# Key/value projections moved between the steps of a pass, and two sample-attention parts joined in one chain

## The chip, the core and the metric

The kernel runs on one core of a Trainium2 chip. The core has five engines that work through their own queues in order and meet at semaphores: TensorE (PE, matrix products and transposes into PSUM), VectorE (DVE), ScalarE (ACT), GpSimd (POOL) and SyncE (SP, which here only issues transfers). PSUM has 8 banks; products land there and ACT or DVE read them out. The metric is the device time of one execution in microseconds (us); the number given for a kernel is the median of its runs.

## The reference, cut to what matters

One inference step of a one-layer decoder is computed for two groups that share their weights: a prompt of 512 rows and eight sample rows, each with 1024 cached rows. All inputs are float32. The mixer, to which the change belongs, computes from the normed rows pooling channels, queries, three branches of keys and values (compressed, selected, window) and gates:

```python
z = rmsnorm(x, g_mix) @ w_in
u = z[..., :o1]
q = z[..., o1:o2].reshape(B, T, N_HEADS, HEAD_DIM)
kv = z[..., o2:o3].reshape(B, T, N_BRANCH, 2, KV_HEADS, HEAD_DIM)
gates = jax.nn.sigmoid(z[..., o3:]).reshape(B, T, N_HEADS, N_BRANCH)
```

Attention over the three branches is weighted by the gates:

```python
p_c = masked_softmax(s_c, cmp_end[None, :] <= pos_q[:, None])     # compressed blocks of 32 rows
imp = jnp.einsum('bghtn,nj->bgtj', p_c, ovl)                      # importance of blocks of 64 rows
_, idx = lax.top_k(imp, k_sel)                                    # 16 blocks, three of them forced
o_s = ...                                                         # softmax over the selected blocks' rows
o_w = jnp.einsum('bghts,bsgd->btghd', p_w.astype(dt), kvw[:, :, 1])   # the last 512 rows
o = g[..., 0:1] * o_c + g[..., 1:2] * o_s + g[..., 2:3] * o_w
```

For the sample rows the cached rows come through a page table, and the selection leaves out one block of 17. After the mixer follow the output projection, cross attention into 256 memory tokens and a gated MLP. The new key and value rows are outputs too.

## The kernel before

Features lie on partitions. The 512 prompt rows and 8 sample rows form the columns of one operand, 2 x 260. To keep float32 accuracy each operand is split into a high and a low part (`split_w`, `split`: ACT copies the high part, line 111, DVE subtracts, line 114), and a projection of 128 output features (`project`, line 194) takes three products for each of 8 row blocks and two column halves: 48 products. Its result gathers in a pair of PSUM banks (`pp`).

The code is Python that is traced once. Generators mark with `yield cost` where another generator may go on, and `merge` runs several side by side in proportion to the costs that they yield. The trace order is a priority. A planner then fixes each engine's order at compile time by priority and by its own estimate of when an instruction's inputs are ready, and places a wait where a buffer is used again (`bufs` counts the buffers of a name). `open_pool` takes space from the left or the right end of SBUF, `open_psum` banks; a new pool over an old one's place waits tile by tile.

The stages around the change, in order:

- Query tiles (`q_tiles`): four projections, beside them the compressed branch's keys and values (`kv_tiles(0)`). Each query tile's result is at once split into `Qst`, eight heads of high and low parts, by ACT and DVE.
- The pass over the cached rows (`sample_pass`): 4 quarters (two batch rows each) of 8 steps. POOL gathers 1 MB of rows for two steps into one of three buffers (`ch_raw`, line 606). In each step `front` reorders them (`chg`), transposes keys (line 613) and the rows to be compressed (line 617), keeps the values (`Vh`) and splits the turned rows (`cx_hi`, `cx_lo`). `back` multiplies the step before with the compressing weights (line 429), accumulating over a quarter in a bank `s`, and every second step computes the selected branch's scores (line 639) into `Ssl`. At the end of a quarter `cmp_finish` reads the bank four times (ACT into `cmp_t`, DVE line 564 into `KC`, `VC`). Banks: two `s`, two `tk`, four `tb`.
- `s1_b` beside `sample_selected`. `s1_b` projects keys and values of the selected and window branches, four tiles; keys are split into `Ksl` and `Kwn` for the prompt's attention, and all are turned back (line 477) and stored. `sample_selected` is a chain: compressed probabilities, the block left out, a softmax over 1025 scores, transposes (line 728), products with the values (line 735).
- `pooling` beside `sample_window`. Pooling has four projections, sums over windows on POOL, four small products (line 840). `sample_window` loads keys and values of the window (`kw` with four buffers, `vw` with eight), turns the keys (line 899), takes scores (line 904), softmax, products (lines 928 and 932), and adds up the sample rows' attention in `ysel`. Its pool lies where `Vh` was.
- The prompt's attention (scores line 976) beside the pooling half of the output projection (line 865) and the memory's projection.

## Time and profile before

| | us |
|---|---|
| median of 3 runs | 923.21 |
| lowest and highest | 921.41, 924.14 |
| span of the profiled execution | 922.6 |
| query tiles, 34.9 to 62.8 | 27.9 |
| pass over the cached rows, 62.8 to 126.6 | 63.8 |
| key/value tiles beside the selected branch, 126.6 to 163.8 | 37.2 |
| pooling beside the window, 163.8 to 207.6 | 43.8 |

The profiled execution's span, from its first to its last instruction, is 0.6 us under the median of the runs. In rows of the profile PE is TensorE's products, PEld its weight loads, which overlap them, and SPq the transfers that SP issues. L194 is line 194 of the kernel. A row of a timeline gives start, duration, engine, line, operation, what is written and read, and in brackets how long the engine idled before and what ended that. A product's duration overlaps that of the next; the pace is the distance of starts. A busy PE therefore isn't a PE at its peak.

### The profile page before, as it was taken

How to read it: one execution, taken by the hardware profiler on the slowest of the kernel's cores; microseconds unless marked ns; L12 is line 12 of the kernel's file. 1: busy time of each engine (PE TensorE's matmuls, PEld its weight loads, DVE VectorE, ACT ScalarE, POOL GpSimd, SP SyncE). 2: the span in 40 equal slices, each digit the busy share in tenths (PEclk: the TensorE clock that was granted, in tenths of full speed). 3: DMA queues.
4: the chain of work that ended last, by engine and by line, in shares of the span. 5: the costliest groups of instructions: out<-in, count | busy, mean ns of one | idle time of the engine just before them, and what ended most of it. 6: DMA issues, size and time to landing. Idle time of an engine off the chain costs nothing.

```text
span 922.6 us, 17866 instructions
## 1 busy us (share of the span) xinstructions
PE 894.8 (97%) x7266; PEld 827.3 (90%) x7266; DVE 610.5 (66%) x1547; ACT 420.8 (46%) x794; POOL 90.5 (10%) x93
## 2 busy tenths in 40 slices
PE   7999999899999999999998999999999999999996
PEld 6997788788878768999888999999999999999995
DVE  5566676558876775788765368775357775357765
ACT  6657764136675665444433344443124443124432
POOL 2112200420000001300004200000000000000051
PEclk9999999999999999999999999999999999999998
DMA  7447753821133336647733453332333332333212
GB/s 206 154 137 267 246 181 100 240 59 49 47 97 110 115 99 185 222 142 247 251 126 100 160 178 106 92 96 91 90 92 92 92 96 92 90 94 93 78 52 93
DMA packets 125460, 118.99 MB, mean 129 GB/s; under 512 B 8985, under 2 KB 116413, under 8 KB 123251
## 3 DMA queue, kind: packets, MB, share of 16 engines
q1 hardware_dynamic: 121523, 94.02, 33.9%
q0 software_dynamic: 3824, 23.80, 7.2%
q8 instruction: 57, 0.93, 0.5%
q14 instruction: 24, 0.20, 0.1%
q10 hardware_dynamic: 32, 0.04, 0.0%
HBM read 111.75 MB, written 10.69 MB: 133 GB/s over the span
## 4 chain that ended last, share of the span: by engine, by line
PE 85%; DMA 7%; DVE 3%; ACT 2%; issue 1%; SPq 0%; DVEq 0%; ACTq 0%
PE ps_pp L194 57%; DMA ch_raw<-in_cache_kv_dram,ix_ch 3%; PE ps_tb L865 3%; PE ps_tb L1103 3%; PE ps_sc L976 3%; PE ps_o L1012 2%; DMA w_u<-in_w_up_dram 2%; PE ps_tb L1130 2%; PE ps_tf L1005 2%; PE ps_s L429 2%; DMA w_kv<-in_w_in_dram 1%; PE ps_x L1289 1%; PE ps_x L1270 1%; PE ps_tb L617 1%; PE ps_tb L639 1%; DVE w_lo L114 1%
## 5 line engine op out<-in xcount | busy, mean ns | idle before, releaser
L194 PE MATMUL ps_pp<-x_hi,w_lo 128*128 128x260 f32 x832 | 169.2, 284 | 0.5 <-DVE w_lo L114 0.5
L194 PE MATMUL ps_pp<-x_hi,w_hi 128*128 128x260 f32 x832 | 169.5, 284 | 0.0
L194 PE MATMUL ps_pp<-x_lo,w_hi 128*128 128x260 f32 x832 | 167.9, 283 | 0.0
L194 PEld LDWEIGHTS ps_pp<-x_hi,w_lo 128*128 128x128 f32 x832 | 128.7, 188 | 1.2 <-DVE w_lo L114 0.7
L194 PEld LDWEIGHTS ps_pp<-x_hi,w_hi 128*128 128x128 f32 x832 | 128.7, 188 | 0.4
L194 PEld LDWEIGHTS ps_pp<-x_lo,w_hi 128*128 128x128 f32 x832 | 128.1, 188 | 0.4 <-issue 0.4
L111 ACT ACTIVATE w_hi<-w_raw 128x1024 fp32r<-128x1024 f32 (+1 forms) x54 | 55.8, 1036 | 114.6 <-PE ps_pp L194 100.9
L114 DVE TENSOR_TENSOR hT<-hT,ps_pp 128x520 f32<-128x520 f32 (+1 forms) x42 | 28.1, 670 | 86.3 <-PE ps_pp L194 83.3
L111 ACT ACTIVATE w_hi<-w_u 128x1024 fp32r<-128x1024 f32 x44 | 46.7, 1061 | 76.0 <-PE ps_pp L194 64.9
L114 DVE TENSOR_TENSOR w_lo<-w_raw,w_hi 128x1024 fp32r<-128x1024 f32 (+1 forms) x54 | 66.7, 1236 | 8.3 <-ACT w_hi L111 8.1
L194 PE MATMUL ps_pp<-h_hi,w_hi 128*128 128x260 f32 x328 | 66.7, 284 | 0.0
L194 PE MATMUL ps_pp<-h_hi,w_lo 128*128 128x260 f32 x328 | 66.0, 282 | 0.0
L194 PE MATMUL ps_pp<-h_lo,w_hi 128*128 128x260 f32 x328 | 66.0, 282 | 0.0
L114 DVE TENSOR_TENSOR ext<-ps_pp,R 128x512 f32<-128x512 f32 x44 | 30.4, 691 | 45.3 <-PE ps_pp L194 45.1
L114 DVE TENSOR_TENSOR w_lo<-w_u,w_hi 128x1024 fp32r<-128x1024 f32 x44 | 53.9, 1226 | 6.8 <-ACT w_hi L111 6.5
L194 PEld LDWEIGHTS ps_pp<-h_hi,w_hi 128*128 128x128 f32 x328 | 50.6, 188 | 0.3 <-ACT h_hi L111 0.2
L194 PEld LDWEIGHTS ps_pp<-h_lo,w_hi 128*128 128x128 f32 x328 | 50.5, 188 | 0.0
L194 PEld LDWEIGHTS ps_pp<-h_hi,w_lo 128*128 128x128 f32 x328 | 50.5, 188 | 0.0
L194 PE MATMUL ps_pp<-xn_hi,w_hi 128*128 128x260 f32 x224 | 48.6, 296 | 0.4 <-ACT xn_hi L327 0.4
L261 POOL TENSOR_TENSOR acc<-hT 128x520 f32<-128x520 f32 x3 | 4.2, 1397 | 456.2 <-DVE hT L114 456.2
L194 PE MATMUL ps_pp<-xn_hi,w_lo 128*128 128x260 f32 x224 | 47.2, 289 | 0.5 <-DVE w_lo L114 0.5
L194 PE MATMUL ps_pp<-xn_lo,w_hi 128*128 128x260 f32 x224 | 46.8, 290 | 0.5 <-DVE xn_lo L330 0.5
(494 smaller groups left out, 2068.0 us busy)
## 6 DMA issues: line engine op xcount, KB each, us to landing
w_u<-in_w_up_dram SPq DMA_DIRECT2D x44, 512.0 KB, 5.3
xkr<-in_cache_mem_dram SPq DMA_DIRECT2D x16, 512.0 KB, 6.3
xvr<-in_cache_mem_dram SPq DMA_DIRECT2D x16, 512.0 KB, 5.1
w_raw<-in_w_down_dram SPq DMA_DIRECT2D x8, 1024.0 KB, 5.0
w_raw<-in_w_in_dram SPq DMA_DIRECT2D x4, 1024.0 KB, 5.3
w_raw<-in_w_xkv_dram SPq DMA_DIRECT2D x4, 1024.0 KB, 5.6
w_v<-in_w_xkv_dram SPq DMA_DIRECT2D x4, 1024.0 KB, 5.8
w_raw<-in_w_xq_dram SPq DMA_DIRECT2D x4, 1024.0 KB, 6.5
```

Source lines behind the costliest of these rows:

```text
L111: act.activation(o, i, AF.Copy, scale=scale)
L114: (eng or dve).tensor_tensor(o, a, b, op=op)
L194: pe.matmul(ps[:, hf, :HT], a[:, k, :], x[:, hf, :], start=(k == 0 and j == 0), stop=(k == kt - 1 and j == 2))
L429: pe.matmul(ps, w[:, c, j].rearrange("p i e -> p (i e)"), x, start=(first and j == 0 and q == 0), stop=(j == 7 and q == 2), skip_group_che ...
L617: pe.transpose(pt[:, a * P:(a + 1) * P], chg[:, a].rearrange("p s d -> p (s d)"), ident)
L639: pe.matmul(ps[32 * c:32 * c + 32, 0:256], Qbd[:, blk(r, c):blk(r, c) + 32], kt[:, i].rearrange("p t n -> p (t n)"), start=True, stop=True ...
L865: pe.matmul(ps[:, :HT], a[:, k, :], y[x][:, k, hf, :], start=(k + j == 0), stop=(k == 3 and j == 2))
L976: pe.matmul(ss_[hl][:, 0:c0 + nk], Qst[:, h, qc], k[:, g, u, 0:c0 + nk], start=(u == 0), stop=(u == 1))
L1005: pe.transpose(pt[:, hh * P:(hh + 1) * P], pr[hh][:, kb * P:(kb + 1) * P], ident)
L1012: pe.matmul(po[hp * 64:(hp + 1) * 64, g * 256:(g + 1) * 256], Vtok[:, br, kb - 1, g * 64:(g + 1) * 64], pTs[kb - 1][:, hp * 256:(hp + 1) * ...
L1103: pe.matmul(ps[:, 0:MEM], a[:, k, :], x[:, k, :], start=(k == 0 and j == 0), stop=(k == 7 and j == 2))
L1130: pe.matmul(ps[i], x[:, k, ts_], w[:, kl, :], start=(k == 0 and j == 0), stop=(k == KT - 1 and j == 2))
```

## The change

The four projections of the selected and the window branch's keys and values leave their own stage. They become `kv_rest`, which is merged with the pass, row block by row block (six products between two yields); the pass yields twice per step. Their weights come by 128 columns into one buffer of the pass's pool. The results stay in `zk` (keys) and `Vtok` (values); the split of the keys comes later (`split_keys`). For their PSUM pair the pass gives up one of its two `s` banks and one of four `tb` banks.

The selected branch, the key splits and the window now form one generator, `samples`, beside `pooling`, which yields after each row block. The window's pool opens when the selected branch is done.

The queries stay unsplit in `zq`; `split_queries` makes `Qst` after pooling, ahead of the prompt's attention. `kv_first` is the compressed branch's part of `kv_tiles`, with its turning in a `tb` bank. Comments are dropped throughout.

```diff
+    Vtok = ptile(at, [P, 2, NQB, P], "Vtok")
...
+    zq = ptile(smp, [P, 4, 2, HT], "zq")
+    zk = ptile(smp, [P, 2, 2, HT], "zk")
...
+    def kv_rest():
+        def load(i):
+            raw = ptile(p0, [P, KT, P], "w_kv")
+            c0 = 1280 + i * P
+            sp.dma_start(raw, w_in[:, c0:c0 + P].rearrange("(k p) c -> p k c", p=P))
+            return raw
+        raw = load(0)
+        for i in range(4):
+            br, c = 1 + i // 2, i % 2
+            w = split_w(raw)
+            if i < 3:
+                raw = load(i + 1)
+            yield 0.3
+            ps = pp()
+            for k in range(KT):
+                project(ps, w, xs1, ks=(k,))
+                yield 0.7
+            z = ztile() if c else zk[:, br - 1]
+            tt(z, ps[:, :, :HT], R1, OP.mult)
             vcopy(zS[:, 2 * br + c, :].rearrange("p (r t) -> p r t", r=2), z[:, :, 256:260])
+            yield 0.3
+            turn_out(z, br, c, Vtok[:, br - 1] if c else ptile(zp[0], [P, NQB, P], "vtr"))
...
-                z = ztile()
+                z = zq[:, x]
                 tt(z, ps[:, :, :HT], R1n, OP.mult)
                 for i in range(2):
                     a, b = halves(i)
                     h = 2 * x + i
-                    q = Qst[:, h, :].rearrange("p (r t) -> p r t", r=2)
-                    acopy(q[a], z[a, :, :256])
-                    tt(q[b], z[a, :, :256], q[a].bitcast(F32), OP.subtract)
...
+    def split_queries():
+        for h in range(8):
+            a, b = halves(h % 2)
+            q = Qst[:, h, :].rearrange("p (r t) -> p r t", r=2)
+            acopy(q[a], zq[a, h // 2, :, :256])
+            tt(q[b], zq[a, h // 2, :, :256], q[a].bitcast(F32), OP.subtract)
+    def split_keys():
+        for br in range(2):
+            for g in range(2):
+                a, b = halves(g)
+                hi = Kst[br][:, g, 0, :].rearrange("p (r t) -> p r t", r=2)
+                lo = Kst[br][:, g, 1, :].rearrange("p (r t) -> p r t", r=2)
+                dup_split(hi, lo, zk[:, br, :, :256], a, b)
+                yield 0.5
...
                 new = (ct, j) + front(ct, j)
+                yield 0.9
                 if prev:
                     back(*prev)
                 prev = new
-                yield 2.1
+                yield 1.2
...
-    es_psa = open_psum("psa", "left", s=2,tk=2,tb=4)
+    es_psa = open_psum("psa", "left", s=1, tk=2, tb=3, pp=1)
     passes = sample_pass()
-    for _ in range(4):
+    for _ in range(8):
         next(passes)
     with last_on(EN.DVE):
         run(gates)
-    run(passes)
+    merge((passes, 58.8), (kv_rest(), 26.0))
...
-    merge((s1_b(), 21.6), (sample_selected(), 21.6))
-    es_pb.close()
-    es_vp.close()
...
-                project(ps, w, xs1)
+                for k in range(KT):
+                    project(ps, w, xs1, ks=(k,))
+                    yield 0.7
...
-    merge((pooling(), 4 * 5.4 + 3.6), (sample_window(), 13.0))
+    def samples():
+        nonlocal pwn
+        yield from sample_selected()
+        es_pb.close()
+        es_vp.close()
+        pwn, es_pwn = open_pool("pwn")
+        yield from split_keys()
+        yield from sample_window()
+        es_pwn.close()
+    merge((pooling(), 4 * 5.6 + 3.6), (samples(), 36.0))
     sample_store()
-    es_pwn.close()
     es_pu.close()
+    at3, es_at3 = open_pool("at3", "right")
+    Qst = ptile(at3, [P, 8, SEQ], "Qst", F32R)
+    split_queries()
     es_smp.close()
```

More of the change, by code (lines that the diff above doesn't have):

```diff
@@ new lines, in turn_out, with kv_first @@
+    def turn_out(z, br, c, v):
+        pt = bank("tb")
+        for n in range(NQB):
+            pe.transpose(pt[:, n * P:(n + 1) * P], z[:, n // 2, (n % 2) * P:(n % 2 + 1) * P], ident)
+        acopy(v.rearrange("p n d -> p (n d)"), pt)
+        sp.dma_start(kv_out[:, :, 2 * br + c, :] if br < 2 else win_out[:, :, c, :], v)
+    def kv_first():
+        z0 = [ztile(), ztile()]
+        for c in range(2):
+            tt(z0[c], ps_kv0[c][:, :, :HT], R1, OP.mult)
+        for c in range(2):
+            z = z0[c]
+            vcopy(zS[:, c, :].rearrange("p (r t) -> p r t", r=2), z[:, :, 256:260])
+            turn_out(z, 0, c, ptile(zp[0], [P, NQB, P], "vtr"))
+            x = ptile(p0, [P, 528], "chg", bufs=2, name="xp_raw").rearrange("p (j x) -> p j x", j=8)
+            for g in range(2):
+                for s in range(2):
+                    src = z[g * 64:(g + 1) * 64, :, :256].rearrange("p r (n j s) -> p r n j s", j=8, s=2)
+                    dst = x[s * 64:(s + 1) * 64, :, g * 32:(g + 1) * 32].rearrange("p j (r n) -> p r n j", r=2)
+                    (vcopy if s == 0 else acopy)(dst, src[:, :, :, :, s])
+            vcopy(x[:, :, 64:66].rearrange("p j i -> p i j"),
+                  vec[:, 36 + c * 16:52 + c * 16].rearrange("p (i j) -> p i j", i=2))
+            with last_on(EN.DVE):
+                split(wc_hi[:, c], wc_lo[:, c], wc_raw[:, c])
+            compress_prompt(c, x)
+            yield 5.4
@@ L620, in front @@
             split(xh, xl, pt)
-            last_split[:] = nc.cur_bb.bb.instructions[-2:]
             return xh, xl, pk[0]
@@ L869, in sample_window @@
     def sample_window():
+        Swn = ptile(pwn, [P, WIN + 1], "Swn")
         kvs = ptile(pwn, [NB, 6 * P], "kvs")
@@ L1166, in decoder_step @@
     es_pq.close()
+    es_at3.close()
     es_at2.close()
```

59 lines of the change are left out of this document (4 added, 55 removed).

## The prediction

> **What bounds the kernel now.** I read the page's busy table first, then the busy time by stage (my own stretches: query tiles, the cached rows' pass, key/value tiles beside the selected branch, pooling beside the window), then the chain of waits, and last the timelines of single engines at the places that the change touches.
>
> ```profile
> span 922.6 us, 17866 instructions
> ...
> PE 894.8 (97%) x7266; PEld 827.3 (90%) x7266; DVE 610.5 (66%) x1547; ACT 420.8 (46%) x794; POOL 90.5 (10%) x93
> ...
> 34.90:62.80 27.90, 27.81 (x234) 27.43 (x233) 18.00 (x45) 11.65 (x28) 2.20 (x2) 1.00 0.40 127
> 62.80:126.60 63.80, 61.38 (x457) 48.37 (x456) 44.70 (x93) 48.53 (x101) 12.28 (x13) 1.00 0.73 248
> 126.60:163.80 37.20, 35.85 (x407) 33.34 (x407) 23.81 (x55) 17.27 (x29) 1.81 (x1) 1.00 0.38 114
> 163.80:207.60 43.80, 40.57 (x366) 34.66 (x365) 25.02 (x63) 11.88 (x19) 14.61 (x12) 0.96 0.49 139
> ```
>
> The columns after the stretch are its length and the busy time of PE, PEld, DVE, ACT and POOL, then the granted clock, DMA share and GB/s. The reader is to see that TensorE (PE) bounds every stage. The three stages that the change rearranges last 63.8 + 37.2 + 43.8 = 144.8 us, and PE's idle time in them is only 2.4 + 1.4 + 3.2 = 7.0 us. The change removes no PE work. Filling holes can therefore win about 7 us at most, while a new hole costs its whole length.
>
> ```profile
> 34.91 16.33 PE ps_pp L194 x136
> ...
> 85.19 6.76 DMA ch_raw<-in_cache_kv_dram,ix_ch
> ...
> 94.00 0.44 PE ps_tb L617 x4
> ...
> 97.25 0.71 PE ps_s L429 x6
> ...
> 102.14 0.22 PE ps_tk L613 x2
> ...
> 105.93 6.56 DMA ch_raw<-in_cache_kv_dram,ix_ch
> ...
> 115.09 0.56 PE ps_tb L639 x4
> ```
>
> These are pieces of the chain of waits: start, length, what. A projection product paces at 16.33 / 136 = 0.12 us. One step of the pass needs 0.71 + 0.44 + 0.22 us and, every second step, 0.56 us for scores: 1.65 us, so 52.8 us for 32 steps. The pass takes 63.8 us; the difference of 11.0 us is the 2.4 us of idle time (two late gathers show above) and the starts of groups that wait a moment on ACT or DVE, which count as busy.
>
> **The change part by part.**
>
> *Four key/value tiles go into the pass.* A tile is 48 products, 48 x 0.12 = 5.8 us, and four transposes, 0.44 us (the price of L617's): 6.2 us, 24.8 us for four. They come in blocks of six products (0.72 us). What they can fill is at least nothing and at most the 11.0 us above. I take half of the idle time, 1.2 us, because the first half of it lies at the pass's start, ahead of the tiles, and because a short wait between two groups is not removed by a third group in the same queue. Pass after: 63.8 + 24.8 - 1.2 = 87.4 us (bounds 77.6 and 88.6). ACT gets a weight split (1.06 us) and a copy (0.60) per tile, DVE a split (1.22) and a multiplication (0.70): 6.6 and 7.7 us on engines that are busy 48.5 and 44.7 us of what becomes 87, so nothing on the path. The rows are groups of instructions: count, busy time in all, mean ns of one, idle time before; the last is a group of loads with its median time to landing.
>
> ```profile
> L111 ACT ACTIVATE w_hi<-w_raw 128x1024 fp32r<-128x1024 f32 x5 | 5.3, 1058 | 9.4 <-PE ps_pp L194 9.4
> ...
> L114 DVE TENSOR_TENSOR w_lo<-w_raw,w_hi 128x1024 fp32r<-128x1024 f32 x6 | 7.3, 1221 | 0.8 <-ACT w_hi L111 0.8
> ...
> L114 DVE TENSOR_TENSOR ztile<-ps_pp,R 128x520 f32<-128x520 f32 x4 | 2.8, 700 | 5.3 <-PE ps_pp L194 5.3
> ...
> L111 ACT ACTIVATE vtr<-ps_tf 128x512 f32<-128x512 f32 x2 | 1.2, 588 | 0.0
> ...
> L111 ACT ACTIVATE Ksl<-ztile 64x512 fp32r<-64x512 f32 x2 | 1.3, 630 | 0.0
> ...
> w_raw<-in_w_in_dram SPq DMA_DIRECT2D x4, 1024.0 KB, 5.3
> ```
>
> *SP and POOL.* Two weight loads of 1 MB become four of 0.5 MB into one buffer. Each waits for the split of the one before (1.06 + 1.22 us) and lands some 5.3 us later by the load group's median; the tile in between spreads over a quarter of the pass, some 20 us, which covers it. Without that cover a tile would begin up to 7.6 us late, but only filler would be late. The four stores of turned rows move on SP's queue with the tiles and wait for nothing that the pass needs. POOL's gathers are passed by nothing new; they get easier, 87.4 / 16 = 5.5 us apart in place of about 4.
>
> *One accumulator bank, three transpose banks, one pair of banks for the tile.* Each quarter of the pass accumulates in bank s, of which there were two.
>
> ```profile
> 95.62 0.28 PE L429 MATMUL ps_s<-cx_hi,wc_lo 128*128 128x256 f32 x1
> ...
> 97.01 0.37 PE L429 MATMUL ps_s<-cx_hi,wc_hi 128*128 128x256 f32 x1
> ...
> 100.81 0.34 DVE L564 SCALAR_TENSOR_TENSOR VC<-ps_s,pec,cmp_t 64x126 f32<-64x126 f32 x1
> ```
>
> The last product of a quarter starts at 95.62, its last reader ends at 101.15, and the next quarter's first product starts in the second bank at 97.01. With one bank it starts 4.1 us later, at three boundaries 12.4 us. Behind that product on PE's queue stand the following steps' products. The cover is the tile blocks, six of which fill 4.3 us, if they are queued ahead of it. I take 0, the lower bound; the upper is 12.4 us.
>
> *Selected branch, key splits and window become one chain beside the pooling tiles.* PE work left there: 35.9 + 40.6 - 24.8 = 51.6 us. The chain:
>
> ```profile
> 137.51 0.22 DVE L686 TENSOR_REDUCE mc<-Pc 128x1 f32<-128x63 f32 x1
> ...
> 142.05 1.08 DVE L114 TENSOR_TENSOR Ssl<-Ssl,imp 128x896 f32<-128x896 f32 x1
> ...
> 148.44 1.21 DVE L673 TENSOR_REDUCE mc<-Ssl 128x1 f32<-128x1025 f32 x1
> ...
> 151.46 1.15 ACT L674 ACTIVATE Ssl<-Ssl,mc 128x1025 f32<-128x1025 f32 x1
> ...
> 153.70 2.31 ACT L111 ACTIVATE S<-Ssl,mc 32x1024 f32<-32x1024 f32 x2 [1.00 <-DVE mc L114]
> ...
> 163.08 0.29 DVE L108 COPY oS<-ps_s 128x128 f32<-128x128 f32 x1 [3.41 <-PE ps_s L735]
> ...
> 164.31 2.10 SPq L895 DMA_DIRECT2D kw<-in_cache_win_dram  x4
> ...
> 173.50 2.39 SPq L895 DMA_DIRECT2D kw<-in_cache_win_dram  x2
> ...
> 181.06 0.92 SPq L895 DMA_DIRECT2D kw<-in_cache_win_dram  x2
> ...
> 192.63 0.60 ACT L111 ACTIVATE Swn<-ps_s 128x512 f32<-128x512 f32 x1 [1.14 <-PE ps_s L904]
> ...
> 205.51 0.41 DVE L108 COPY oS<-ps_s 128x256 f32<-128x256 f32 x1
> ...
> 207.63 1.03 PE L976 MATMUL ps_sc<-Ksl,Qst 128*128 128x416 f32 x4 [0.60 <-ACT ut L111]
> ```
>
> Own time of its first part: finishing the blocks 1.3 us, selection 5.5 (137.51 to 143.13, less a 0.70 multiplication of a tile in between, with 0.6 for product and copy ahead), softmax 6.0 (1.21, 1.15, 2.31 and small ones), transposes and values 7.0 up to 163.08: 19.8 us; before it took 36.5. From there to the window's first load 1.2 us. Own time of the window: the loads come in three rounds since keys have four buffers; I estimate 13.5 us for two rounds and 5.5 for the last with its scores, then 8.5 for the softmax and values (192.63 to 205.92 holds 13.3): 27.5 us; before it took 43.3 up to the first score product. The first window load waits for the last read of the selected values, as before. The key splits, four of 2 x 0.63 us on ACT, come while these loads land, so I take 0.5 us; the bounds are 0 and, without that cover, 5 us. Of the 16.7 + 15.8 us of waiting in the two parts, a good half was behind 48-product tiles on PE's queue, which become 0.72 us blocks; the rest, behind tile work on DVE, thins out because four tiles now stand beside the whole chain instead of eight. I keep a quarter, 8 us (bounds 0 and 32.5). Chain: 19.8 + 1.2 + 27.5 + 8 = 56.5 us, more than its 51.6 us of PE work. So the chain, not PE, sets this stage.
>
> *Query splits.* Eight splits move from beside the query tiles, where PE was busy 27.8 of 27.9 us and they cost nothing, to behind the pooling tiles.
>
> ```profile
> L114 DVE TENSOR_TENSOR Qst<-ztile,Qst 64x512 fp32r<-64x512 f32 x8 | 5.5, 686 | 1.1 <-ACT Qst L111 0.9
> ...
> L111 ACT ACTIVATE Qst<-ztile 64x512 fp32r<-64x512 f32 x8 | 5.0, 627 | 1.8 <-DVE ztile L114 1.7
> ```
>
> Pooling's PE work ends before the chain does, so the window's tail covers most of them; I take one ACT copy and its hop, 0.7 us (bounds 0 and 6.2, one copy and then DVE's whole group). Taking them out of the query stage gains nothing there. The other new tiles (zq, zk) only change where a result is put.
>
> *Sum.* 87.4 + 56.5 + 0.5 + 0.7 = 145.1 us against 144.8: span 922.9 us. The median of the runs, 923.2, stands 0.6 over the profiled span of before: **923.5 us**, no change that can be measured. Filler was moved out of the stages whose chain needed it, into one that PE already filled.
>
> **The rivals.**
>
> *B, faster: PE sets both stages.* Both idle rests go: 63.8 + 24.8 - 2.4 = 86.2, and the chain fits under its 51.6 us of PE work, 7.0 us in all less: 916. For it: the chain's own time is 48.5 us. Against it: it needs waits under 3.1 us over some forty steps.
>
> *C, slower: the single bank.* Half of the 12.4 us remains unfilled: 929.7; all: 935.9. It decides from 3 us on. For it: each boundary shows the late readers. Against it: tile blocks are ready most of the time. In a sentence apart: the Trainium skill, "TensorE: Matmul & The Clock Gate", section "Step-by-step: what each phase is for", says that products stay in program order and only weight loads are pulled ahead; a product that waits for the bank would then hold every block queued behind it.
>
> *D, slower: the chain keeps half of its waits and PE's clock drops.* 16.3 us of waits in place of 8: 8.3 us more, 931.8; from 3 us more on it decides.
>
> ```profile
> 170.00:172.00 2.00, 1.03 (x9) 0.82 (x7) 2.00 (x2) 0.00 (x0) 1.92 (x2) 1.00 1.15 293
> 172.00:174.00 2.00, 0.90 (x6) 0.69 (x6) 2.00 (x5) 0.00 (x0) 1.99 (x4) 1.00 0.79 196
> 174.00:176.00 2.00, 1.62 (x8) 1.62 (x9) 1.45 (x3) 0.42 (x1) 1.42 (x2) 0.50 0.48 138
> 176.00:178.00 2.00, 2.00 (x13) 2.00 (x13) 0.49 (x4) 0.18 (x1) 0.00 (x0) 0.64 0.56 166
> ```
>
> After 4 us in which PE was busy half the time the granted clock was 0.50, and back at 1.00 some 3.4 us later. With less filler in a chain-bound stage such places become more. The Trainium skill, "TensorE: Matmul & The Clock Gate", section "What's actually happening", gives half clock after one idle window of about 3.4 us; by it two dips would add an estimated 3.4 us, 927. The trace agrees on the length, but its dip came with PE only half idle, which is worse.
>
> **How the numbers follow.** Forecast (918 to 929) 0.40; B 0.25; C 0.18; D 0.17. About 0.3%, 2.8 us, is what a measurement of this kernel can tell from no change. Of the forecast's case 0.10 falls under 920.4, 0.17 within, 0.13 above; of B 0.24 faster; of C and D 0.31 slower and 0.04 within. Faster 0.34, same 0.22, slower 0.44. The range runs from below B's time, 912, to D's, 932; it leaves the fully unfilled bank out.
>
> **What would show it.** Right: a pass of 86 to 89 us with PE almost never idle; then a stage of 55 to 60 us in which PE idles 5 to 8 us, waiting for the sample chain; score products that start within 1 us of the window's last copy. Wrong: a pass under 84 us (fill better than I think) or compressing products waiting on the block's finishing at the quarters (C); a second stage of 52 us with PE full (B), or over 63 us with the clock at 0.5 more than once (D); score products waiting on the query splits for several us.

## The result, and the profile after

The changed kernel takes 937.45 us (median of four runs, 936.23 to 938.45) against 922.31 us (920.99 to 924.14) for the kernel before on the same chips: 1.0162 times as long, with a 95% interval of 1.0142 to 1.0181, or about 15 us slower. The forecast was 923.5 us. The profiled execution took 937.33 us; its span is 935.6 us, of which 935.6 - 922.6 = 13.0 us are new.

First the busy table of the page, then the busy time by stage: the query tiles, the pass, the sample chain beside pooling up to its last sums, and from there to the first score product. After the length stand the busy times of PE, PEld, DVE, ACT and POOL, the granted clock, the DMA share and GB/s.

```profile
span 935.6 us, 17841 instructions
...
PE 898.3 (96%) x7266; PEld 829.5 (89%) x7266; DVE 609.8 (65%) x1547; ACT 420.8 (45%) x794; POOL 91.3 (10%) x93
```

```profile
34.00:61.90 27.90, 27.90 (x237) 27.73 (x236) 13.72 (x38) 8.20 (x22) 1.92 (x2) 1.00 0.40 127
61.90:152.20 90.30, 85.67 (x665) 74.17 (x664) 54.25 (x108) 53.57 (x107) 12.60 (x13) 0.98 0.63 204
152.20:213.00 60.80, 51.46 (x557) 43.27 (x556) 36.91 (x98) 20.76 (x37) 16.43 (x13) 0.94 0.42 118
213.00:220.80 7.80, 6.35 (x49) 5.62 (x48) 4.88 (x17) 4.04 (x9) 1.02 (x2) 1.00 0.03 7
```

PE has as many products as before (x7266), and its busy time is 3.5 us longer though no work was added; the granted clock, 0.94 in the third row, goes with that. The miss is where these rows leave the forecast: the pass 90.3 in place of 87.4 (+2.9), the chain 60.8 in place of 57.0 with the key splits (+3.8), then 7.8 in place of 0.7 us to the first score product (+7.1); the query stage ended 0.9 us earlier than before. These add up to 12.9 us. From the first score product to the end it is 935.6 - 220.8 = 714.8 us, before 922.6 - 207.6 = 715.0: by this mark the loss lies ahead of the attention. In the 7.8 us PE isn't idle: 40 of its 49 products there are the output projection's, which before the change ran beside the attention. The places are seen in the timeline:

```profile
61.23 0.37 SPq L487 DMA_DIRECT2D w_kv<-in_w_in_dram  x1
...
65.17 1.06 ACT L111 ACTIVATE w_hi<-w_kv 128x1024 fp32r<-128x1024 f32 x1 [2.44 <-DMA w_kv<-in_w_in_dram]
66.25 1.09 ACT L111 ACTIVATE cx_hi<-ps_tb 128x512 fp32r<-128x512 f32 x2
...
66.90 0.39 PE L430 MATMUL ps_s<-cx_hi,wc_hi 128*128 128x256 f32 x1 [2.41 <-ACT cx_hi L111]
...
150.87 0.37 SPq L872 DMA_DIRECT2D w_op<-in_w_out_dram  x1
151.29 0.55 SPq L801 DMA_DIRECT2D stp<-in_state_pool_dram  x1
...
158.96 0.63 PE L804 MATMUL ps_tf<-cst,stp 120*128 120x120 f32 x4 [3.23 <-DMA stp<-in_state_pool_dram]
...
173.10 0.69 DVE L840 SCALAR_TENSOR_TENSOR pl_d<-pl_s,U 128x512 f32<-128x512 f32 x1 [2.31 <-POOL pl_s L114]
...
180.52 2.79 PE L750 MATMUL ps_tb<-cst,S 128*128 128x128 f32 x12 [3.18 <-DVE S L744]
...
213.04 1.01 DVE L114 TENSOR_TENSOR ysel<-ps_tb,oSel 64x8 f32<-64x8 f32 x8 [0.84 <-PE ps_tb L955]
...
213.72 0.60 PE L860 MATMUL ps_tf<-cst,ulast 128*24 128x128 f32 x4
...
218.61 0.63 ACT L111 ACTIVATE w_hi<-w_op 128x512 fp32r<-128x512 f32 x1 [3.31 <-PE ps_tb L880]
219.15 5.19 ACT L111 ACTIVATE Qst<-zq 64x512 fp32r<-64x512 f32 x8
...
220.83 0.61 PE L992 MATMUL ps_sc<-Ksl,Qst 128*128 128x416 f32 x2 [0.23 <-DVE Qst L114]
```

The reader is to see waits that have one form: an engine's queue is in order, and its first instruction waits for something that the work behind it doesn't need. The second weight load (61.23) waits for the first weight split, as there is one buffer; ACT's split of it (65.17) waits for the load, and the pass's own split `cx_hi`, queued behind, lets PE stand 2.41 us. On SP's queue pooling's state rows `stp` stand behind the output projection's weights `w_op`, which wait for a buffer; they then land 7.6 us after their issue, where the same load landed in 3.9 us before the change. PE stands 3.23 us, with the chain's next product queued behind. DVE waits for POOL's sums (173.10) with the chain's softmax behind it, and PE stands again at 180.52. At the end the first query copy (219.15) stands on ACT behind a weight split that waits 3.31 us for output projection products, and the first score product waits for the query splits. The clock behind the stop at the pass's start, and beside the two in the chain's stage:

```profile
67.00:71.00 4.00, 4.00 (x22) 4.00 (x23) 2.28 (x4) 2.00 (x4) 0.94 (x1) 0.59 1.06 330
156.00:160.00 4.00, 1.04 (x9) 1.05 (x10) 3.11 (x12) 3.88 (x8) 0.00 (x0) 0.98 0.41 94
160.00:164.00 4.00, 4.00 (x21) 3.44 (x20) 2.42 (x8) 0.13 (x1) 0.00 (x0) 0.59 0.00 0
176.00:180.00 4.00, 0.38 (x2) 0.12 (x2) 3.40 (x9) 3.79 (x5) 3.63 (x3) 1.00 0.00 0
180.00:184.00 4.00, 3.48 (x16) 2.78 (x17) 2.85 (x8) 0.77 (x2) 0.00 (x0) 0.57 0.08 6
```

Behind each stop the granted clock is near one half for most of 4 us. The rows at 160 and 180 us lack 4 x 0.41 + 4 x 0.43 = 3.4 us of full clock, the row at 67 us another 4 x 0.41 = 1.6 us. By how much that lengthens the time these rows don't show.

### The profile page after: what moved, and what is told of

The parts are those of the page before. It is cut to its first block, busy times and chain, and to the rows that moved or that the text cites. A ratio compares the mean times of both kernels' runs of the same rounds, so it can differ in the third digit from the quotient of the medians.

```text
span 935.6 us, 17841 instructions
## 1 busy us (share of the span) xinstructions
PE 898.3 (96%) x7266; PEld 829.5 (89%) x7266; DVE 609.8 (65%) x1547; ACT 420.8 (45%) x794; POOL 91.3 (10%) x93
## 4 chain that ended last, share of the span: by engine, by line
PE 80%; DMA 8%; DVE 5%; ACT 3%; issue 3%; POOL 1%; SPq 0%; DVEq 0%; ACTq 0%; POOLq 0%
PE ps_pp L194 53%; PE ps_tb L1119 2%; DMA ch_raw<-in_cache_kv_dram,ix_ch 2%; PE ps_o L1028 2%; DMA w_u<-in_w_up_dram 2%; PE ps_tb L1146 2%; PE ps_sc L992 2%; PE ps_tb L880 2%; PE ps_tf L1021 2%; DMA w_kv<-in_w_in_dram 2%; PE ps_s L430 2%; PE ps_x L1318 1%; PE ps_x L1299 1%; ACT w_hi L111 1%; DVE w_lo L114 1%
## 5 line engine op out<-in xcount | busy, mean ns | idle before, releaser
L111 ACT ACTIVATE w_hi<-w_raw 128x1024 fp32r<-128x1024 f32 (+1 forms) x50 | 51.7, 1034 | 101.8 <-PE ps_pp L194 86.3
L114 DVE TENSOR_TENSOR w_lo<-w_raw,w_hi 128x1024 fp32r<-128x1024 f32 (+1 forms) x50 | 60.5, 1209 | 7.9 <-ACT w_hi L111 7.7
L194 PE MATMUL ps_pp<-xn_hi,w_hi 128*128 128x260 f32 x224 | 50.6, 306 | 0.5 <-ACT xn_hi L327 0.4
```

What stands on the lines that cost most here:

```text
L111: act.activation(o, i, AF.Copy, scale=scale)
L114: (eng or dve).tensor_tensor(o, a, b, op=op)
L194: pe.matmul(ps[:, hf, :HT], a[:, k, :], x[:, hf, :], start=(k == 0 and j == 0), stop=(k == kt - 1 and j == 2))
```

## The experiments

All ratios are to the kernel before, run on the same chip; "us against the changed kernel" are differences of ratios times 922.

### One part alone: the late query splits

The kernel before, with `zq` and `split_queries` and nothing else of the change:

```diff
+    zq = ptile(smp, [P, 4, 2, HT], "zq")
...
-                z = ztile()
+                z = zq[:, x]
...
     es_pu.close()
+    at3, es_at3 = open_pool("at3", "right")
+    Qst = ptile(at3, [P, 8, SEQ], "Qst", F32R)
+    split_queries()
```

> The kernel before with one part of the change alone: queries unsplit in zq, split behind pooling and window. Theory 'exposed splits': sixteen operations (eight of 0.63 us on ACT, eight of 0.69 us on DVE in step) come between the window's last sums and the scores, some 5 to 7 us late, less up to 0.9 us from the query stage: 926 to 928.5. The forecast's step was 0.7 us: 922.5 to 923.5. Between these two this run decides.

Measured: 927.5 us, ratio 1.0063 (1.0043 to 1.0083): 5.8 us for this part alone, where the forecast had 0.7. In its trace the first score product starts 3.85 us behind the start of the last sums, before 0.18 us ahead of it. Its timeline at the end of the window:

```profile
206.93 0.99 DVE L114 TENSOR_TENSOR ysel<-ps_tb,oSel 64x8 f32<-64x8 f32 x8
...
209.37 5.21 ACT L111 ACTIVATE Qst<-zq 64x512 fp32r<-64x512 f32 x8 [1.09 <-DMA out_pool_sample_dram<-ut]
210.04 5.71 DVE L114 TENSOR_TENSOR Qst<-zq,Qst 64x512 fp32r<-64x512 f32 x8 [0.92 <-ACT Qst L111]
210.78 0.65 PE L980 MATMUL ps_sc<-Ksl,Qst 128*128 128x416 f32 x2
```

No split ran beside the window's tail. `Qst` lies where pooling's pool `pu` was, and the first copy waited until pooling's last small store, out of a tile `ut` of that pool, had landed. Then the eight splits of each engine take 5.2 and 5.7 us, and the first reductions of the attention queue behind them on DVE. The query stage gains 0.1 us: in this trace the pass starts at 62.7 us, before at 62.8.

### Undoing half of it: heads 0 to 3 early

The changed kernel, with the half of the heads that the first score products read split at once; the other half stays late (the gates' small tile `gx` moves to another buffer for room).

```diff
-                z = zq[:, x]
+                z = ztile() if x < 2 else zq[:, x - 2]
...
+                    if x < 2:
+                        split_query(h, z[a, :, :256])
...
-        for h in range(8):
+        for h in range(4, 8):
```

> The changed kernel with the query heads 0 to 3, which the first score products read, split beside the query tiles again, as before the change; heads 4 to 7 stay late. Theory 'exposed splits': in the changed kernel the first score product comes 7.8 us after the sample chain's last operation began, where it came 0.2 us before it in the kernel before, because sixteen split operations and their place behind pooling's buffers stand in between. Half of them gone and the first reads served: first score product within 1.5 us of the chain's end, time 5 to 7 us under the changed kernel's 937.5, so 930.5 to 932.5; the query stage gets its 0.9 us back, which is in that sum. Rival 'late chain': the attention is held by what surrounds it (the clock, the output projection's weights), and the splits only fill a gap that exists anyway: 936 to 938.

Measured: 932.84 us, ratio 1.0115 (1.009 to 1.014), 4.3 us against the changed kernel. In its trace the chain's last sums start at 214.61 and the first score product at 216.70:

```profile
214.61 1.00 DVE L114 TENSOR_TENSOR ysel<-ps_tb,oSel 64x8 f32<-64x8 f32 x8 [0.84 <-PE ps_tb L961]
...
216.70 1.02 PE L998 MATMUL ps_sc<-Ksl,Qst 128*128 128x416 f32 x4 [0.81 <-ACT ut L111]
```

The 7.8 us became 2.1, and a copy of pooling's last rows, no longer a split, ends the wait. The exposed splits are shown by both runs. The gain in time, 4.3 us, is under the expected 5 to 7; the chain's last sums start 1.6 us later in this trace than in the changed kernel's.

### The pass: weight buffers and accumulator banks

First two buffers for the weights (the gates' `gx` moves here too):

```diff
-            raw = ptile(p0, [P, KT, P], "w_kv")
+            raw = ptile(p0, [P, KT, P], "w_kv", bufs=2)
```

> The changed kernel with two buffers for the key/value weights of the pass instead of one (a 12 KB tile of the gates moves into another buffer to make room). Theory 'split ahead of the step': the second weight load waits for the first split, ACT's second split waits 2.44 us for that load at 65.17 us, and the pass's own splits are queued behind it, so that TensorE stands 2.57 us. With two buffers the wait goes: time 934.5 to 936, the pass 87.5 to 88.5 us in place of 90.3. Rival: TensorE's loss of 2.9 us against the forecast of the pass comes from the single accumulator bank: 937 to 938, pass 90 us.

Measured: 935.11 us, ratio 1.0151 (1.0123 to 1.0179), not to be told from the changed kernel by time. The trace shows the step itself:

```profile
62.10:150.00 87.90, 84.94 (x666) 72.76 (x665) 53.97 (x108) 53.00 (x108) 12.32 (x13) 1.00 0.63 205
```

The pass lasts 87.9 us and the stop at its start is gone, so it was ACT's queue behind the load that made it. The halved clock at 67 us is gone with it. The span is only 1.4 us shorter; the chain behind the pass took 1.4 us more.

Then two accumulator banks:

```diff
-    es_psa = open_psum("psa", "left", s=1, tk=2, tb=3, pp=1)
+    es_psa = open_psum("psa", "left", s=2, tk=2, tb=2, pp=1)
```

> The changed kernel with two accumulator banks and two transpose banks in the pass, instead of one and three. Theory 'blocks fill the boundary': the six microseconds between two quarters' products are filled by tile blocks, so the second accumulator brings 0 to 1 us, and the transpose bank that is given up costs something: 937 to 940. Rival 'single bank' (C of the forecast): the pass gains 3 us or more: 931 to 934.5.

Measured: 934.35 us, ratio 1.0137 (1.0114 to 1.016), 2.3 us against the changed kernel, with intervals that overlap; it lies at the upper end of the rival's range. But where its span is shorter, it isn't by the bank: from its first transpose to the last compressing product the pass takes 89.7 us (62.2 to 151.9), in the changed kernel 90.4 (61.9 to 152.4), each with a stop and a halved clock at its start. The rest lies behind it, at the state's transposes:

```profile
157.33 0.63 PE L804 MATMUL ps_tf<-cst,stp 120*128 120x120 f32 x4 [2.02 <-DMA stp<-in_state_pool_dram]
```

```profile
156.00:164.00 8.00, 6.67 (x51) 6.20 (x52) 7.12 (x25) 4.66 (x9) 0.47 (x1) 1.00 0.15 31
```

The stop is 2.02 us in place of 3.23, and the clock stays at 1.00 in these 8 us, where the changed kernel had 0.59 in the second half of them.

### The state load, by two ways

First into a place of its own, issued ahead of the pass:

```diff
+    stp = ptile(smp, [120, 512], "stp")
+    sp.dma_start(stp, A["state_pool"][0].rearrange("b t c -> (b t) c"))
     vp, es_vp = open_pool("vp")
```

> The changed kernel with pooling's state rows (0.24 MB) loaded into a place of their own ahead of the pass, instead of behind the waiting weight load on SP's queue. In the changed kernel TensorE stands 3.23 us at the state's transposes (158.96 us), with the sample chain's and pooling's products queued behind. Theory 'load behind a blocked queue': these 3.2 us go, time 934 to 935.5. Rival: the chain has its next wait right behind (DVE behind POOL at 173 us), and takes the 3 us back there: 937 to 938.

Measured: 947.21 us, ratio 1.0277 (1.0257 to 1.0297), a miss for both. In its trace the pass starts 7.3 us later, at 69.2 us, from a place that has nothing to do with pooling. A copy of the first gathered rows came ahead of the compressed branch's work on DVE, PE stopped 2.46 us, and the clock was halved for some 9 us while PE was full:

```profile
32.41 0.76 DVE L108 COPY Vh<-ch_raw 128x256 f32<-128x256 f32 x1 [2.16 <-DMA ch_raw<-in_cache_kv_dram,ix_ch]
...
33.91 1.12 PE L458 MATMUL ps_tb<-cst,ztile 128*128 128x128 f32 x4 [2.46 <-DVE ztile L114]
```

```profile
34.00:36.00 2.00, 1.90 (x8) 1.52 (x9) 1.96 (x5) 0.56 (x1) 0.00 (x0) 0.50 0.00 0
...
42.00:44.00 2.00, 2.00 (x12) 2.00 (x12) 0.97 (x5) 0.77 (x4) 0.00 (x0) 0.55 0.87 192
```

For the question of the state load the time is inconclusive. In the trace the state's transposes no longer wait, but PE stops 3.06 us for the next product of the chain, and the chain is as long as in the changed kernel: 60.9 us from the last compressing product to the last sums (161.6 to 222.5), there 60.8. The second way changes the queue alone:

```diff
-        sp.dma_start(stp, A["state_pool"][0].rearrange("b t c -> (b t) c"))
+        pool.dma_start(stp, A["state_pool"][0].rearrange("b t c -> (b t) c"))
```

> The changed kernel with the load of pooling's state rows issued from POOL's queue, where it stands behind the last gather alone, in place of SP's, where it stands behind the weight load that waits for a buffer; the place of the tile stays. In the changed kernel TensorE stands 3.23 us at the state's transposes. Theory 'load behind a blocked queue': the load lands some 5 us or more earlier, the stop goes, and the chain's next products come 2.5 to 3 us earlier, as they did in the run with two accumulator banks, where the load landed 1.7 us earlier: 933.5 to 935.5. Rival 'taken back': the chain's next wait (key splits ahead of it on ACT and DVE) swallows it: 936.5 to 938.

Measured: 937.11 us, ratio 1.0168 (1.0138 to 1.0199): nothing gained, the rival's number. The state's transposes no longer wait (they run at 156.72), but the next product of the chain does, for probabilities that DVE scales behind the key splits, and the clock is halved for longer than in the changed kernel:

```profile
160.68 0.43 PE L714 MATMUL ps_tb<-cst,Pc 128*63 128x128 f32 x2 [1.95 <-DVE Pc L712]
```

```profile
162.00:168.00 6.00, 6.00 (x28) 5.73 (x27) 3.77 (x11) 1.06 (x1) 1.33 (x2) 0.51 0.00 0
```

### Both stops gone

The same, and the key splits kept behind the chain's first exponential on ACT and DVE:

```diff
-                dup_split(hi, lo, zk[:, br, :, :256], a, b)
+                with last_on(EN.Activation, EN.DVE):
+                    dup_split(hi, lo, zk[:, br, :, :256], a, b)
```

> The changed kernel with the state load on POOL's queue, as in the run before, and in it also the key splits held behind the first exponential of the chain on ACT and DVE, instead of ahead of it. With the load alone moved, TensorE stopped 1.95 us at line 714 and its clock was 0.50 from 162 to 168 us. Theory 'clock': both stops gone, the clock stays at 1.00 there, and the selected branch ends 3 us earlier (33 us behind the last compressing product in place of 35.7): 933 to 935. Rival 'the chain's own order': the splits move between the probabilities and the next operations of the chain and take from it what they gave: 936 to 938.

The clock in this kernel, where the changed kernel has its first two waits of the chain:

```profile
156.00:164.00 8.00, 7.03 (x65) 6.15 (x64) 5.10 (x24) 1.26 (x5) 1.29 (x1) 1.00 0.44 148
160.00:168.00 8.00, 7.97 (x75) 7.47 (x76) 6.32 (x16) 3.59 (x6) 2.53 (x2) 1.00 0.01 1
```

The clock stays at 1.00 up to 168 us, and the selected branch ends 30.8 us behind the last compressing product (155.4 to 186.2) in place of 35.7 (152.4 to 188.1): the theory's part. The stop ahead of the softmax's transposes is still there (3.17 us, to 178.4 us). Stop, halved clock and key splits went together, so the 4.9 us aren't told apart. But the last compressing product itself comes 3.0 us later, and the whole is 935.03 us, ratio 1.016 (1.0142 to 1.0177), as slow as the changed kernel. The trace shows where the pass gave that back: it starts 0.8 us later, and its last quarter is 2.4 us longer. There ACT waits for pooling's first weights, with the pass's own split queued behind.

```profile
147.17 1.06 ACT L111 ACTIVATE w_hi<-w_raw 128x1024 fp32r<-128x1024 f32 x1 [4.03 <-DMA w_raw<-in_w_in_dram]
...
148.76 0.38 PE L430 MATMUL ps_s<-cx_hi,wc_hi 128*128 128x256 f32 x1 [1.16 <-ACT cx_hi L111]
```

In the changed kernel the same wait of ACT is 1.57 us and no stop of PE follows. With the state load alone moved it is 3.55 us, so it isn't the key splits that make it long; what does isn't shown.

### DVE behind POOL

Pooling's differences `pl_d` go one tile later, behind the next tile's products:

```diff
+                if todo:
+                    finish(*todo.pop())
                 u = ptile(pu, [P, 536], "U", bufs=2)
...
-                d = ptile(pu, [P, 2, HT], "pl_d", bufs=4)
...
+                todo.append((gi, win, u, cur))
```

> The changed kernel with pooling's differences (pl_d, line 840 and the five operations behind it) traced one tile later, behind the next tile's products, with a third buffer for the window sums. In the changed kernel DVE waits 2.31 us at 173.10 us for POOL's sums, and the chain's copy and reduction (174.06 us), whose scores were there at about 169 us, are queued behind. Theory 'DVE behind POOL': the wait loses the chain, its softmax starts 3 to 4 us earlier, and TensorE's 3.18 us stop at 180.5 us shrinks: 933 to 935. Rival 'chain's own length': the products before and the transposes behind set the chain, another operation takes the same place: 936.5 to 938.

Measured: 939.5 us, ratio 1.0195 (1.0171 to 1.0219), 3.0 us slower than the changed kernel, with intervals that overlap. The order by priority put `pl_d` in the same place ahead of the chain's reduction, so the wait stayed, and PE's stop ahead of the softmax's transposes grew from 3.18 to 4.97 us. The experiment didn't remove what it was to remove; what that wait costs stays open.

### The chain by itself

The chain traced wholly ahead of pooling (`run(samples())`, then `run(pooling())`), and then, in a second kernel, pooling also held until the chain's last operation:

```diff
-    merge((pooling(), 4 * 5.6 + 3.6), (samples(), 36.0))
+    run(samples())
+    with last_on(EN.DVE):
+        run(pooling())
```

> The changed kernel with the sample chain traced wholly ahead of the pooling tiles, so that it has the priority on every engine, and pooling only fills. Theory 'the chain is held by filler': of the 60.8 us from the last compressing product to the chain's last operation some 4 to 8 us are waits behind pooling's work; they go, but pooling's tail comes behind the chain: chain 52 to 56 us, time 932 to 940. Rival 'own length': the chain stays at 59 to 61 us with everything out of its way, so its own operations were under-counted by the forecast.

> The changed kernel with pooling held back until the sample chain's last operation, so that the chain runs with nothing beside it: a measurement of its own length. The forecast counted 48.5 us of own time and 8 us of waits; in the changed kernel the chain takes 60.8 us from the last compressing product to its last operation. If the count holds, the chain takes 48 to 51 us here; if its own time was under-counted, 54 to 60 us. The time of the whole is some 30 us above the changed kernel and says nothing.

With priority the chain takes 56.8 us (154.7 to 211.5), just over the theory's 52 to 56, but the scores start at 224.2 us, since pooling's tail comes behind it: 936.47 us, ratio 1.0157 (1.0131 to 1.0183). With nothing beside it (a single run of 956.97 us in all, with pooling's work behind the chain):

```profile
152.80:204.70 51.90, 32.68 (x359) 21.17 (x358) 20.48 (x53) 16.09 (x30) 2.89 (x3) 0.76 0.34 91
```

51.9 us at a clock of 0.76, against 48.5 counted; it lies between the two ranges expected, nearer to the first. So the chain's own time was counted nearly right, and 60.8 - 51.9 = 8.9 us are what the work beside it costs, near the 8 us of the forecast. How much of the 8.9 us is clock this doesn't tell: the chain alone ran at a lower clock than the chain with work beside it.

### Where the tiles stand

Only the selected branch's two tiles in the pass; the window branch's two ahead of pooling, beside the chain:

```diff
-    merge((passes, 58.8), (kv_rest(), 26.0))
+    merge((passes, 58.8), (kv_rest((0, 1)), 13.0))
...
+    def filler():
+        yield from kv_rest((2, 3), True)
+        yield from pooling()
+    merge((filler(), 12.4 + 4 * 5.6 + 3.6), (samples(), 36.0))
```

> The changed kernel with only the selected branch's two tiles between the pass's steps; the window branch's two tiles stand ahead of pooling's, beside the chain. Theory 'filler in the wrong stage': the chain's stage lasts 68.6 us to the first score product while it holds 51.6 us of TensorE's work, so 12.4 us more of filler cost it only 0 to 4 us, and the pass becomes 10 to 12.4 us shorter: 925 to 931. Rival 'the chain is pushed back': each block beside the chain makes it later by its own length, so the time stays at 936 to 938.

Measured: 930.46 us, ratio 1.0096 (1.0065 to 1.0127), 6.1 us against the changed kernel. The pass and the chain up to its last sums:

```profile
62.60:141.20 78.60, 72.10 (x564) 60.16 (x566) 50.80 (x101) 50.41 (x104) 12.61 (x13) 1.00 0.66 215
141.20:208.10 66.90, 61.12 (x659) 54.42 (x658) 42.01 (x105) 23.88 (x40) 16.30 (x13) 0.97 0.45 131
```

The chain's stage takes up two tiles, 12.4 us of PE work, for 66.9 - 60.8 = 6.1 us, and the pass gets 11.7 us shorter. In this trace neither of the chain's stops of over 3 us is left: the place of the softmax's transposes is filled, and the state load is now issued at 140.4 us, ahead of `w_op`, and has landed when its transposes run. So the gain is the filler's and the state load's together; they aren't told apart. With half the tiles in the pass the single accumulator bank shows at a quarter's end:

```profile
126.83 0.39 PE L430 MATMUL ps_s<-cx_hi,wc_hi 128*128 128x256 f32 x1 [1.14 <-DVE VC L587]
```

With the repairs of the queries (heads 0 to 3 early) and of the pass's start (the second weight split placed behind the pass's own) in it (two small tiles, `zv` and `ut`, also share other buffers for room):

```diff
+            with (last_on(EN.Activation, EN.DVE) if i == 1 else ExitStack()):
+                w = split_w(raw[:, :, c * P:c * P + P] if win else raw)
```

> The kernel with two tiles in the pass and two beside the chain, and in it also: heads 0 to 3 split beside the query tiles, and the pass's second weight split placed behind the pass's own splits on ACT and DVE. Theory 'three separate costs add up': the two-tile kernel's 930.5 less 4 us (queries) less 2 us (TensorE's stop at 66 us): 923 to 926, no better than the kernel before by more than can be measured. Rival 'one bottleneck': the stage's end is set by pooling's tail or the output projection's weights, so the parts don't add: 927 to 931.

Measured: 925.82 us, ratio 1.0039 (1.0026 to 1.0051). It wins 11.3 of the 15 us and is the best of the versions that keep the change; it is still 3.6 us slower than the kernel before, and no version here beats that one.

With four tiles in the pass, as the change has it, and four repairs (heads 0 to 3 early, the state load on POOL's queue, the key splits held, the second weight split behind the pass's own; the edits are those above):

> The changed kernel with all four tiles in the pass, as the change has it, and four repairs: heads 0 to 3 split beside the query tiles, the state load on POOL's queue, the key splits held, the pass's second weight split placed behind the pass's own. Theory 'waits, not places': the gains add up, 937.4 - 4.4 - 3 - 1.5 = 928.5, so 926.5 to 930.5. Theory 'place of the tiles': it stays some 3 us or more above the kernel with two tiles and two repairs (925.8), 929 to 933, since the chain's stage has too little filler. Below 926 the tiles' place would not matter at all.

Measured: 927.89 us, ratio 1.0084 (1.0067 to 1.0101). The repairs win 7.2 us together; by their ratios alone they won 4.3 (queries), 1.0 (two weight buffers, another way to the same end) and 0.2 us (state load and key splits). It stays 4.1 us above the kernel with two tiles, and the intervals don't meet. But one of the four repairs didn't take:

```profile
148.76 0.59 POOL L809 DMA_DIRECT2D stp<-in_state_pool_dram  x1 [17.82 <-PE ps_s L431]
...
154.81 0.63 PE L812 MATMUL ps_tf<-cst,stp 120*128 120x120 f32 x4 [2.75 <-DMA stp<-in_state_pool_dram]
```

On POOL's queue the state load now waits until the pass's last compressing product has run, and PE stands 2.75 us again, with the chain's probabilities ready behind. The kernel with two tiles has no such stop. So this pair of runs doesn't decide between waits and places. Its profiled execution was the shortest of its four (924.68 us):

```profile
62.50:148.50 86.00, 83.95 (x665) 72.51 (x664) 54.05 (x108) 52.70 (x108) 12.28 (x13) 1.00 0.66 215
148.50:206.70 58.20, 50.88 (x558) 42.39 (x557) 39.06 (x104) 21.47 (x37) 16.23 (x14) 0.97 0.43 123
206.70:208.20 1.50, 0.69 (x6) 0.32 (x4) 1.46 (x6) 1.25 (x4) 0.00 (x0) 1.00 0.00 0
```

These are 145.7 us, near the forecast's sum of 145.1. That is chance: the pass filled 2.6 us where the forecast took 1.2, and the chain still has two stops, the one above and one of 3.18 us ahead of the softmax's transposes. The mean clock of the other three executions was 0.988 to 0.992 against 0.994 here.

### Row blocks alone

The kernel before, with yields after each row block and everything in its old stage:

```diff
-                project(ps, w, xs1)
+                for k in range(KT):
+                    project(ps, w, xs1, ks=(k,))
+                    yield 0.65
```

> The kernel before with one part of the change alone: the key/value and pooling tiles yield after each row block of six products instead of after 48, everything in its old stage. The forecast's step was that a good half of the sample chain's waits lies behind 48-product tiles. If that holds, the waits shrink, but TensorE idles only 1.4 and 3.2 us in these stages, so the time is 919 to 922. Rival 'no bound': TensorE's work sets these stages and the planner places products by readiness anyway: 921 to 923.5.

Measured: 923.91 us, ratio 1.0023 (1.0011 to 1.0035), slightly slower and above both ranges. The chain's first reduction in its timeline:

```profile
130.43 0.22 DVE L688 TENSOR_REDUCE mc<-Pc 128x1 f32<-128x63 f32 x1
```

It comes 7 us earlier than before (137.51), so 48-product tiles did hold the chain. But the score products start at 207.5 us, before at 207.6: in this trace PE's work sets these stages, and a chain that is earlier has nothing to win there.

## Why the prediction was wrong

**The step that failed first** is "Pooling's PE work ends before the chain does, so the window's tail covers most of them". The query splits were put at 0.7 us (bounds 0 and 6.2); they cost 5.8 us alone, and 7.1 us more than forecast in the changed kernel's trace. The sixteen operations were priced by their durations, but not by when they may begin: `Qst` lies over pooling's tiles, and pooling's last reader is as late as the chain: in the changed kernel pooling's last transposes on PE (213.72) start behind the chain's last sums (213.04), and a copy and a store follow them. Nothing of the tail is left for the splits. In the changed kernel ACT's queue adds a weight split ahead of them. The prediction had named this sign itself: score products that wait on the query splits for several us. The upper bound was near; the value was taken at the wrong end.

**The second** is "a tile would begin up to 7.6 us late, but only filler would be late". The waiting instruction wasn't followed by filler: on ACT the pass's own split stood behind it. The size was 2.4 us of stop and a halved clock behind it, and the pass came out at 90.3 us, outside its bounds of 77.6 to 88.6; two buffers took both away and brought it to 87.9.

**The chain's stage.** It missed its 57.0 us by 3.8. Its own time (48.5 counted, 51.9 with nothing beside it at a lower clock) and the sum of its waits (8 counted, 8.9 measured) came out near. That 48-product tiles held the chain was right, as the run with row blocks alone shows. What was missed is other waits: behind the state load, POOL's sums and the key splits. Of the moved DMAs only the weights and stores were counted; that the state load of 0.24 MB stands on SP behind a load that waits for a buffer was missed, and the key splits at 0.5 us were priced without what waits behind them. With both out of the way the selected branch ended 4.9 us earlier behind the pass, more than the whole miss of the stage. No term of the sum held the clock. Rival D named it with "two dips would add an estimated 3.4 us", and the trace has two in this stage and one in the pass. But D's price went by 16.3 us of waits and its sign was a second stage of over 63 us; 60.8 us and 8.9 us of waits bear out its clock and not its waits. What the clock costs by itself no run here separates.

**What held.** The single accumulator bank costs next to nothing while all four tiles fill behind it (the pass with two is 0.7 us shorter), so rival C falls. A pass of 63.8 + 24.8 us less what is filled is what the traces show without the stop: 87.9 with two weight buffers and 86.0 with four repairs, 0.7 and 2.6 us filled where 1.2 were taken. That the query stage gains nothing is nearly right: the pass starts at 62.7 us with the queries late alone, and between 61.9 and 62.7 us in all others but the one with the early state load, before at 62.8. Rival B needed waits under 3.1 us; they were 8.9. The last sentence of the sum, that filler was moved out of the stages whose chain needed it, is borne out in part: two tiles put back win 6.1 us, but the state load's stop went with them.

**The clock rule.** In the changed kernel three stops, of 2.41, 3.23 and 3.18 us, are each followed by some 3.4 us near half clock. The Trainium skill, "TensorE: Matmul & The Clock Gate", section "HAM oscillation — how this bites in real kernels", states as its rule that idle gaps of TensorE over about 3.4 us are to be avoided. These runs are less kind: single stops of 1.95, 2.41 and 2.46 us were followed by a halved clock, while one of 2.02 us and one of 2.75 us were not. The measurement decides here: gaps well under that figure can cost.

**What stays open:** what the clock, the state load's stop and the tiles' place cost by themselves, why pooling's first weights came late in two of the kernels with the state load on POOL's queue, and what DVE's wait for POOL costs by itself.

## What to carry to other kernels

Before a load, a split or a copy is priced at nothing, name the instruction that stands behind it on its own queue, and the last reader of the memory that it will write: both set when it begins, and its duration alone doesn't. In a stage that is set by a dependent chain TensorE needs filler: with none beside the chain its clock was 0.76, and behind stops of 2 to 3 us it was often halved. A repair is to be looked for in its own trace: the state load, put on another queue, once ran free and once waited for another reader. And a repaired stop is worth its time only if the next one on the chain isn't already waiting: of the stops repaired here one by one, only that of the queries gave a gain beyond its interval.

## What the runs showed of the hardware

The granted clock isn't a matter of the stop's length alone: after 2.02 us (two accumulator banks) and after 2.75 us (four repairs) it stayed at 1.00, after 1.95 us it was near 0.5 for some 7 us, after 2.46 us for some 9 us, in the last two with PE all but full. We had expected it back some 3.4 us later, as the row of the kernel before had it. The stop at the pass's start shows it at one and the same place: after 2.05 us in the kernel with the chain traced first (first row), and after 2.26 us in the kernel with the state load on POOL's queue (second row). What else decides isn't shown.

```profile
67.00:73.00 6.00, 5.90 (x27) 5.86 (x27) 2.84 (x5) 2.81 (x6) 0.94 (x1) 0.50 1.01 345
```

```profile
67.00:73.00 6.00, 5.78 (x45) 5.05 (x46) 4.71 (x8) 4.52 (x10) 0.94 (x1) 1.00 0.99 321
```

DVE is slower while POOL adds. The same addition of the chosen blocks takes 1.98 us in the changed kernel, where POOL begins its sums at the same time, and 1.09 us with the key splits held, where POOL begins 2.3 us later. The timelines of the changed kernel, then of the other:

```profile
166.62 1.06 POOL L114 TENSOR_TENSOR pl_s<-U 128x527 f32<-128x527 f32 x1 [12.40 <-DVE imp L724]
...
166.65 1.98 DVE L114 TENSOR_TENSOR Ssl<-Ssl,imp 128x896 f32<-128x896 f32 x1
```

```profile
163.13 1.09 DVE L114 TENSOR_TENSOR Ssl<-Ssl,imp 128x896 f32<-128x896 f32 x1
...
165.39 1.07 POOL L114 TENSOR_TENSOR pl_s<-U 128x527 f32<-128x527 f32 x1 [8.10 <-ACT w_hi L111]
```

The difference, 0.89 us, is nearly the length of one POOL addition. The Trainium skill, "SBUF — State Buffer", section "Terms", says that VectorE and GpSimd share a pair of ports, held for a whole instruction, so that the loser waits; the two rows agree with it. Joining the chain with pooling therefore also made an operation of the chain itself longer, which the forecast took from a stage without POOL (1.08 us).
